# Four residual layers on one Trainium2 core: the norm's row factors inside the first early product, modulation products in groups of four, short fetches elsewhere

## The chip, the core and the metric

The kernel runs on one core of a Trainium2 chip. The metric is the time of one execution in device microseconds. Three runs of the kernel before took 2492.18, 2496.58 and 2499.11 us; the median is 2496.58 us. One further execution was profiled, and all rows below come from it.

## The reference

Four layers work on 256 tokens of 1024 channels; the first two also carry 256 context tokens. Every layer is a mixer and then a gated FFN of width 2816, each behind a modulated RMS norm, with a gated residual sum:

```
m = split(silu(c) @ mod_w[layer] + mod_b[layer], 6)      # shift, scale, gate; shift, scale, gate
h = rms_norm(x, g) * (1 + scale) + shift
x = x + gate * mixer(h)
x = x + gate2 * ((silu(h2 @ w_gate) * (h2 @ w_up)) @ w_down)
```

The mixers are: attention beside a gated linear recurrence (even), retention (odd), and twice a gated delta rule beside window attention, with short convolutions; the FFN of those two has a convolution as well. All is in 32-bit floats. The first two layers need the modulation for two vectors (c and c_ctx), the last two for one.

## The kernel before

A planner orders the work. The program emits instructions with priorities (earlier is more urgent; `high_priority` and `urgent()` raise it, a negative value lowers it), and the planner, with its own costs, puts them into the queues of the engines. Each engine works its queue in order. Nearly all fetches are issued by SyncE, in order, and rotate over eight semaphores; a fetch waits until the one that used its semaphore eight fetches earlier has landed.

**Weights.** `wload` (171) fetches 128 x 1024 floats into one of four `raw` buffers. ScalarE rounds it into `whi` (181), and VectorE, or at every `pool_every`-th load GpSimd, forms the remainder `wlo` (183). A product is three matmuls per block, `mm3` (187 to 192): high x high, low x high, high x low. At the end `wload` calls `fill` (184), which adds `rate` to a credit and, for each whole credit, takes one piece of the modulation from `self.todo`.

**Modulation.** There are three ways. For the first layer's shift and scale, `modulate_first` (1057) multiplies on TensorE at the start. For the rest of the first layer, `mod_round` (337) fetches 128 x 512 floats into one of three `mraw` buffers for each of 8 k and 4 column groups, and multiplies each at once, the 4 groups into 4 different 32-row strips of one bank; it is emitted with low priority in the even mixer. For the other three layers, `mod_sums` (350) does the sum over k as 280 multiply-adds on VectorE (363), after a first scaling on ScalarE (365), and ends each column group with one matmul per vector that sums over the partitions (369). One `yield` is one piece; there are 288. `rate` is 2.9 per weight load in the even layer's FFN, 1.5 in the odd mixer and 1.0 in the odd FFN. `mod_cols` (381) adds the bias and turns the row into columns.

**Norms.** The output product of each part goes channel block by channel block, n = 0 to 7. `norm_block` (504) squares the block on ScalarE (520), adds it to `nsum` on GpSimd (524), and writes the block, scaled but not yet normalized, into hT (527, 528). `norm_scale` (530) then sums over channels with matmuls (537, 538), takes the power -1/2 (540, 541), puts it on a diagonal (545), spreads it to all partitions with matmuls (546) and copies it to `nrs` (548). Meanwhile one or two early products run on the unnormalized hT (`deferred`, 550, with 258 columns, two of them for the shift); their results are multiplied by `nrs` afterwards (`scaled`, 565). `normed` (577) then writes the normalized h over hT in 8 blocks: multiply (587), add the shift and round on ScalarE (588), remainder (589). There are seven such norms after the first one. Squares, scaled results and the products of line 587 share the ring `nt` of five buffers.

**Short fetches.** The head gains `qkg` are fetched at the start (1050), ahead of the vectors (1061), the bias (1068) and the first modulation weights (1078). `swa_heads` (1404 to 1406) and `Delta.gates` (1615, 1616) fetch five small vectors each in each of the last two layers.

Of the kernel before, what the change touches and what calls it, by code (L numbers as in the profile page):

```python
# [19 lines left out]
P = 128  # L20
# [76 lines left out]
class Net:  # L97
# [73 lines left out]
    def wload(self, srcs, a, b):  # L171
# [165 lines left out]
    def mod_round(self, M, r):  # L337

        nc = self.nc
        w, cond = M["w"], self.cond  # L340
        pa = self.bank("mod")
        for k in range(8):
            for g in range(4):
                raw = self.t(self.mpool, [P, 512], tag="mraw", bufs=3)
                c0 = r * 2048 + g * 512
                nc.sync.dma_start(raw, w[k * P:k * P + P, c0:c0 + 512])
                nc.tensor.matmul(pa[32 * g:32 * g + 32], lhsT=cond[:, k, :], rhs=raw, start=k == 0, stop=k == 7)
        self.mod_cols(M, r, pa, range(M["nm"]))

    def mod_sums(self, M, r):  # L350

# [3 lines left out]
        for g in range(4):  # L355
            accs = [self.t(self.mod_pool, [P, 512], tag=f"macc{m}", bufs=1) for m in range(len(vs))]
            for k in range(8):
                raw = self.t(self.mod_pool, [P, 512], tag="mraw2", bufs=2) if k % 5 > 2 else self.t(self.mpool, [P, 512], tag="mraw", bufs=3)
                c0 = r * 2048 + g * 512
                nc.sync.dma_start(raw, M["w"][k * P:k * P + P, c0:c0 + 512])  # L360
                for v, acc in zip(vs, accs):
                    if k:
                        nc.vector.scalar_tensor_tensor(acc, raw, v[:, k:k + 1], acc, ALU.mult, ALU.add)  # L363
                    else:
                        nc.scalar.activation(acc, raw, AF.Copy, scale=v[:, 0:1])  # L365
                if k < 7:
                    yield
            for m, acc in enumerate(accs):
                nc.tensor.matmul(pa[32 * g:32 * g + 32], lhsT=self.ones[:, m], rhs=acc, start=m == 0, stop=m == len(accs) - 1)
            if g == 3:  # L370
                self.mod_cols(M, r, pa, range(len(vs)))
# [9 lines left out]
    def mod_cols(self, M, r, pa, ms):  # L381
# [3 lines left out]
        row = self.t(self.mpool, [P, 512], tag="modrow", bufs=1)  # L385
# [47 lines left out]
    def out_proj(self, y, w, x, gates, rows=None, kbs=None, follow=False, send=None, late=False):  # L433
# [35 lines left out]
        if follow:  # L469
            with self.urgent():  # L470
                self.norm_scale()
# [32 lines left out]
    def norm_block(self, n):  # L504
# [12 lines left out]
        for m, x in enumerate(self.nx):  # L517
            s = slice(m * 256, m * 256 + 256)
            sq = self.t(self.npool, [P, 256], tag="nt", bufs=5) if n else self.nsum[:, s]
# [3 lines left out]
            elif n:  # L523
                nc.gpsimd.tensor_tensor(self.nsum[:, s], self.nsum[:, s], sq, ALU.add)
# [5 lines left out]
    def norm_scale(self):  # L530

        nc, mm = self.nc, self.nc.tensor.matmul
        nt = 2 * len(self.nx)
        ps = self.sm()
        for i in range(nt):
            o = ps[:, 2 * i:2 * i + 2]
            mm(o, lhsT=self.nsum[:, i * P:i * P + P], rhs=self.ones2, start=True, stop=False)
            mm(o, lhsT=self.nsq[i // 2][:, i % 2 * P:i % 2 * P + P], rhs=self.ones2, start=False, stop=True)
# [3 lines left out]
        diag = self.t(self.npool, [P, nt * P], tag="nsum", bufs=1).rearrange("p (i t) -> p i t", t=P)  # L542
        pb = self.sm()
        for i in range(nt):
            nc.vector.tensor_scalar(diag[:, i], self.ident, rs[:, i:i + 1], None, ALU.mult)
# [1359 lines left out]
```

## Time and profile before

| | |
|---|---|
| profiled execution | 2499.45 us |
| its span, first to last instruction | 2497.7 us |
| TensorE (PE) busy | 2372.8 us, 95% |
| VectorE (DVE) busy | 1600.4 us, 64% |
| ScalarE (ACT) busy | 1066.2 us, 43% |
| GpSimd (POOL) busy | 714.9 us, 29% |
| read from HBM | 389.27 MB, 157 GB/s over the span |

A busy TensorE is a pipelined one: neighbouring matmuls overlap in the records, so the shares add up as unions. PEclk is the share of TensorE's clock that was granted. Plain 32-bit matmuls, as in the modulation, leave two records each, the three of `mm3` one each. "Idle before" names what ended an engine's wait.

### The profile page before, as it was taken

How to read it: one execution, taken by the hardware profiler on the slowest of the kernel's cores; microseconds unless marked ns; L12 is line 12 of the kernel's file. 1: busy time of each engine (PE TensorE's matmuls, PEld its weight loads, DVE VectorE, ACT ScalarE, POOL GpSimd, SP SyncE). 2: the span in 40 equal slices, each digit the busy share in tenths (PEclk: the TensorE clock that was granted, in tenths of full speed). 3: DMA queues.
4: the chain of work that ended last, by engine and by line, in shares of the span. 5: the costliest groups of instructions: out<-in, count | busy, mean ns of one | idle time of the engine just before them, and what ended most of it. 6: DMA issues, size and time to landing. Idle time of an engine off the chain costs nothing. (4 is left out here: it accounts for less than half of the span.)

```text
span 2497.7 us, 41691 instructions
## 1 busy us (share of the span) xinstructions
PE 2372.8 (95%) x16388; PEld 2029.3 (81%) x16388; DVE 1600.4 (64%) x2615; ACT 1066.2 (43%) x1744; POOL 714.9 (29%) x537
## 2 busy tenths in 40 slices
PE   6989999999999999998998999998999899999999
PEld 4766658677777788878997887798999787789999
DVE  2676738855656766658545788358765777537773
ACT  2545424332233433334444554235445563345443
POOL 1453423110112112214443453124123352224121
PEclk8999999999999999999998999999999999999999
DMA  7423344566666457556654542245556443245554
GB/s 245 132 89 111 99 132 146 158 198 215 212 219 194 141 174 231 178 181 207 213 178 142 158 122 83 83 140 165 178 183 182 125 134 95 90 139 169 159 180 144
DMA packets 355498, 394.66 MB, mean 158 GB/s; under 512 B 39037, under 2 KB 290861, under 8 KB 355301
## 3 DMA queue, kind: packets, MB, share of 16 engines
q1 hardware_dynamic: 353124, 391.86, 50.9%
q8 instruction: 129, 2.11, 0.3%
q14 instruction: 69, 0.56, 0.1%
q10 hardware_dynamic: 2176, 0.13, 0.1%
HBM read 389.27 MB, written 2.65 MB: 157 GB/s over the span
## 5 line engine op out<-in xcount | busy, mean ns | idle before, releaser
L181 ACT CAST whi<-raw 128x1024 fp32r<-128x1024 f32 (+2 forms) x536 | 553.1, 1033 | 692.4 <-PE acc L191 489.5
L183 DVE TENSOR_TENSOR wlo<-raw,whi 128x1024 fp32r<-128x1024 f32 (+1 forms) x385 | 499.9, 1300 | 375.8 <-ACT whi L181 366.4
L190 PE MATMUL acc<-hTh,whi 128*128 128x256 f32 (+2 forms) x2256 | 695.2, 310 | 20.7 <-ACT hTh L588 15.2
L191 PE MATMUL acc<-hTl,whi 128*128 128x256 f32 (+2 forms) x2256 | 698.4, 310 | 4.6 <-DVE hTl L589 4.4
L192 PE MATMUL acc<-hTh,wlo 128*128 128x256 f32 (+2 forms) x2256 | 696.5, 309 | 1.4 <-DVE wlo L183 1.4
L183 POOL TENSOR_TENSOR wlo<-raw,whi 128x1024 fp32r<-128x1024 f32 (+1 forms) x151 | 363.3, 2406 | 1100.1 <-ACT whi L181 985.6
L190 PEld LDWEIGHTS acc<-hTh,whi 128*128 128x128 f32 x2256 | 433.5, 193 | 59.5 <-ACT hTh L588 16.7
L191 PEld LDWEIGHTS acc<-hTl,whi 128*128 128x128 f32 x2256 | 432.7, 192 | 34.5 <-issue 6.5
L192 PEld LDWEIGHTS acc<-hTh,wlo 128*128 128x128 f32 x2256 | 432.3, 192 | 30.2 <-issue 9.2
L363 DVE SCALAR_TENSOR_TENSOR macc<-mraw,sil,macc 128x512 f32<-128x512 f32 x280 | 233.5, 841 | 48.7 <-ACT macc L365 34.6
L191 PE MATMUL acc<-hidl,whi 128*128 128x256 f32 (+1 forms) x704 | 218.4, 311 | 0.0
L190 PE MATMUL acc<-hidh,whi 128*128 128x256 f32 (+1 forms) x704 | 217.8, 311 | 0.0
L192 PE MATMUL acc<-hidh,wlo 128*128 128x256 f32 (+1 forms) x704 | 217.7, 310 | 0.0
L190 PE MATMUL acc<-whi,hTh 128*128 128x512 f32 (+2 forms) x496 | 182.9, 372 | 13.3 <-ACT hTh L588 12.6
L191 PE MATMUL acc<-wlo,hTh 128*128 128x512 f32 (+2 forms) x496 | 182.5, 369 | 0.0
L192 PE MATMUL acc<-whi,hTl 128*128 128x512 f32 (+2 forms) x496 | 176.7, 366 | 0.0
L190 PEld LDWEIGHTS acc<-hidh,whi 128*128 128x128 f32 x704 | 132.2, 188 | 12.0 <-ACT whi L181 3.4
L191 PEld LDWEIGHTS acc<-hidl,whi 128*128 128x128 f32 x704 | 132.6, 188 | 9.2 <-issue 1.7
L192 PEld LDWEIGHTS acc<-hidh,wlo 128*128 128x128 f32 x704 | 132.6, 188 | 7.8
L190 PEld LDWEIGHTS acc<-whi,hTh 128*128 128x128 f32 x496 | 95.3, 192 | 38.2 <-ACT hTh L588 13.2
L191 PEld LDWEIGHTS acc<-wlo,hTh 128*128 128x128 f32 x496 | 95.5, 193 | 22.4 <-issue 8.0
L192 PEld LDWEIGHTS acc<-whi,hTl 128*128 128x128 f32 x496 | 94.2, 192 | 20.9 <-issue 5.6
(528 smaller groups left out, 3872.9 us busy)
## 6 DMA issues: line engine op xcount, KB each, us to landing
raw<-in_w_in_dram SPq DMA_DIRECT2D x112, 512.0 KB
mraw<-in_w_ada_dram SPq DMA_DIRECT2D x192, 256.0 KB
raw<-in_ffn_w_in_dram SPq DMA_DIRECT2D x88, 512.0 KB
raw<-in_w_up_dram SPq DMA_DIRECT2D x88, 512.0 KB
mraw<-in_mod_w_dram SPq DMA_DIRECT2D x160, 256.0 KB
raw<-in_odd_w_in_dram SPq DMA_DIRECT2D x48, 512.0 KB
raw<-in_ffn_w_out_dram SPq DMA_DIRECT2D x40, 512.0 KB
raw<-in_w_down_dram SPq DMA_DIRECT2D x40, 512.0 KB
```

The lines of the kernel that those rows point to most:

```text
L181: nc.scalar.copy(hi, raw)
L183: eng.tensor_tensor(lo, raw, hi.bitcast(F32), ALU.subtract)
L190: mm(out, lhsT=ah, rhs=bh, start=start, stop=False)
L191: mm(out, lhsT=ah, rhs=bl, start=False, stop=False)
L192: mm(out, lhsT=al, rhs=bh, start=False, stop=stop)
L363: nc.vector.scalar_tensor_tensor(acc, raw, v[:, k:k + 1], acc, ALU.mult, ALU.add)
```

## The change

The norm's row factors are no longer formed at the end of the output product but inside the first early product of the next part: the sums are placed behind its k = 3, the spread behind its k = 7 (`after` adds an order on the queue, without a semaphore). The squares, the scaled results and the products of line 587 get rings of their own (2, 3 and 4 buffers), and the add of block 6 moves from GpSimd to VectorE. Both kinds of modulation products are issued in groups of four that write the four strips of a bank, tied together by `abreast`; `mod_round` fetches 1 MB per k into one buffer, and `mod_sums` has four accumulators and four fetch buffers. `fill` is called by every `mm3` and counts columns, 2048 to a piece, times a rate of 1.3, 1.0 and 1.0. The qkg fetch moves behind the third quarter of the first modulation, the ten small vectors to `setup2`, which runs in the odd layer's FFN. In the odd mixer, the tiles that are first needed after the norm go to a pool that is opened there, `dec` among them. In the last two mixers every second weight remainder goes to GpSimd, up to the values.

```diff
@@ wload, mm3
-        self.fill()
         return hi, lo
...
-        mm(out, lhsT=al, rhs=bh, start=False, stop=stop)
+        last = mm(out, lhsT=al, rhs=bh, start=False, stop=stop)
+        self.fill(int(np.prod(bh.shape[1:])))
+        return last
@@ modulation
+    def after(self, a, b):
+        self.tc.add_manual_dep(a.ins, b.ins.name, mybir.DependencyInfo(mybir.DependencyClass.NoSync, mybir.DependencyReason.DATA), reason="order")
+        return a
+    def abreast(self, mms):
+        last = None
+        for mm in mms:
+            if last is None:
+                last = mm()
+            else:
+                with self.tc.high_priority():
+                    last = self.after(mm(), last)
-    def mod_round(self, M, r):
+    def mod_round(self, M, r, pool):
...
-            for g in range(4):
-                raw = self.t(self.mpool, [P, 512], tag="mraw", bufs=3)
-                c0 = r * 2048 + g * 512
-                nc.sync.dma_start(raw, w[k * P:k * P + P, c0:c0 + 512])
-                nc.tensor.matmul(pa[32 * g:32 * g + 32], lhsT=cond[:, k, :], rhs=raw, start=k == 0, stop=k == 7)
+            raw = self.t(pool, [P, 2048], tag="mraw", bufs=1)
+            nc.sync.dma_start(raw, w[k * P:k * P + P, r * 2048:r * 2048 + 2048])
+            self.abreast([lambda g=g: nc.tensor.matmul(pa[32 * g:32 * g + 32], lhsT=cond[:, k, :], rhs=raw[:, g * 512:g * 512 + 512], start=k == 0, stop=k == 7)
+                          for g in range(4)])
...
+        step = 4 // len(vs)
+        for g0 in range(0, 4, step):
+            gs, accs = range(g0, g0 + step), {}
+            for g in gs:
+                for m in range(len(vs)):
+                    accs[g, m] = self.t(self.mod_pool, [P, 512], tag="macc", bufs=4)
+                for k in range(8):
+                    raw = self.t(self.mod_pool, [P, 512], tag="mraw", bufs=4)
...
+                    if k < 7 or g < gs[-1]:
+                        yield
+            for m in range(len(vs)):
+                self.abreast([lambda g=g: nc.tensor.matmul(pa[32 * g:32 * g + 32], lhsT=self.ones[:, m], rhs=accs[g, m], start=m == 0, stop=m == len(vs) - 1)
+                              for g in reversed(gs)])
...
-    def fill(self):
-        self.credit += self.rate
-        while self.credit >= 1:
-            self.credit -= 1
+    def fill(self, cols):
+        self.credit += self.rate * cols
+        while self.credit >= 2048:
+            self.credit -= 2048
             next(self.todo, None)
@@ out_proj, norm_block, deferred
         if follow:
-            with self.urgent():
-                self.norm_scale()
+            self.nrs = None
...
-            sq = self.t(self.npool, [P, 256], tag="nt", bufs=5) if n else self.nsum[:, s]
+            sq = self.t(self.npool, [P, 256], tag="nsq", bufs=2) if n else self.nsum[:, s]
...
-                nc.gpsimd.tensor_tensor(self.nsum[:, s], self.nsum[:, s], sq, ALU.add)
+                (nc.vector if n == 6 else nc.gpsimd).tensor_tensor(self.nsum[:, s], self.nsum[:, s], sq, ALU.add)
...
+            first = self.nrs is None
...
-                    self.mm3(pa, wh[:, s], wl[:, s], hi[:, k, c], lo[:, k, c], k == 0, k == 7)
+                    last = self.mm3(pa, wh[:, s], wl[:, s], hi[:, k, c], lo[:, k, c], k == 0, k == 7)
+                if first and k in (3, 7):
+                    with self.urgent():
+                        (self.norm_sums if k == 3 else self.norm_spread)(last)
...
-        u, wb = self.t(self.npool, [P, 256], tag="nt", bufs=5), self.col(1, "wb")
+        u, wb = self.t(self.npool, [P, 256], tag="nu", bufs=3), self.col(1, "wb")
...
-                    t = self.t(self.npool, [P, 256], tag="nt", bufs=5)
+                    t = self.t(self.npool, [P, 256], tag="nt", bufs=4)
@@ norm_scale becomes norm_sums (lines 537 to 545) and norm_spread (546 to 548)
+            mm = nc.tensor.matmul(o, lhsT=self.nsum[:, i * P:i * P + P], rhs=self.ones2, start=True, stop=False)
+            self.after(mm, before)
+            before = nc.tensor.matmul(o, lhsT=self.nsq[i // 2][:, i % 2 * P:i % 2 * P + P], rhs=self.ones2, start=False, stop=True)
...
+            mm = nc.tensor.matmul(pb[:, i * P:i * P + P], lhsT=self.onesq, rhs=self.ndiag[:, i], start=True, stop=True)
+            if i == 0:
+                self.after(mm, before)
@@ layer_even, modulate_first
-        for i, n0, n1 in ((0, 0, 8), (1, 8, 10)):
-            self.nc.sync.dma_start(self.qkg[:, n0:n1], I["attn_qk_norm_g"][0, i].unsqueeze(0).unsqueeze(0).to_broadcast([P, n1 - n0, 64]))
...
+            if q == 2:
+                for i, n0, n1 in ((0, 0, 8), (1, 8, 10)):
+                    nc.sync.dma_start(self.qkg[:, n0:n1], I["attn_qk_norm_g"][0, i].unsqueeze(0).unsqueeze(0).to_broadcast([P, n1 - n0, 64]))
@@ odd, setup2, mixer2, swa_heads
+                        o2 = es.enter_context(tc.tile_pool(name="od2", bufs=1, reuse_waits="tile"))
...
+        self.vec2 = [{nm: self.bcast_rows(cp, I[f"{src}_2"][l], w, f"{nm}{l}")
+                      for nm, src, w in (("sgq", "swa_q_norm", 64), ("sgk", "swa_k_norm", 64), ("ssink", "swa_sinks", 16),
+                                         ("alog", "dn_a_log", 8), ("dtb", "dn_dt_bias", 8))} for l in range(2)]
...
+            self.pool_every = 2
...
+                self.pool_every = 4
```

## Rows read from the trace of the kernel before

**Rows 1.** The page, first line: the span.

```profile
span 2497.7 us, 41691 instructions
```

**Rows 2.** Windows: stretch, width, engines' busy us (instructions), PEclk, DMA share, GB/s.

```profile
470.00:830.00 360.00, 360.00 (x1555) 277.54 (x1555) 218.61 (x298) 110.21 (x157) 53.03 (x34) 1.00 0.63 203
```

**Rows 3.** Waits of TensorE: waiter, releaser, total us, times, longest us.

```profile
PE acc L190 <- ACT hTh L588: 27.8, 7, 4.7
PE mod L1083 <- DMA mbig<-in_mod_w_dram: 14.8, 3, 12.9
PE mod L347 <- DMA mraw<-in_mod_w_dram: 2.7, 1, 2.7
```

**Rows 4.** Windows around the seven norms: width, PE busy (instructions), PEclk, DMA share, GB/s.

```profile
435.00:445.00 10.00, 5.46 (x11) 0.66 0.56 177
...
838.00:848.00 10.00, 6.45 (x25) 0.83 0.64 187
1138.00:1165.00 27.00, 20.64 (x123) 0.81 0.51 157
1340.00:1374.00 34.00, 22.04 (x133) 0.80 0.35 98
1736.00:1746.00 10.00, 4.71 (x23) 0.66 0.34 105
1933.00:1944.00 11.00, 6.36 (x18) 0.69 0.29 75
2307.00:2319.00 12.00, 6.70 (x33) 0.72 0.28 88
```

**Rows 5.** TensorE's timeline, 1717 to 1742 us: start, length, what, [idle before].

```profile
1723.23 0.28 PE L190 MATMUL acc<-hTh,whi 128*128 128x258 f32 x1
...
1740.85 0.80 PE L190 MATMUL acc<-hTh,whi 128*128 128x256 f32 x2 [4.60 <-ACT hTh L588]
```

**Rows 6.** VectorE's timeline, 405 to 470 us and 1717 to 1745 us.

```profile
441.65 1.27 DVE L589 SCALAR_TENSOR_TENSOR hTl<-nt,modcols,hTh 128x256 fp32r<-128x256 f32 x3
...
1734.24 0.75 DVE L569 TENSOR_TENSOR nt<-acc,nrs 128x256 f32<-128x256 f32 x2 [1.92 <-ACT nrs L548]
...
1739.79 0.47 DVE L587 SCALAR_TENSOR_TENSOR nt<-x,moda,nrs 128x256 f32<-128x256 f32 x1
```

**Rows 7.** TensorE's timeline, 68 to 110 us and 296 to 352 us.

```profile
76.01 1.06 PE L347 MATMUL mod<-mraw,cond 128*32 128x512 f32 x6
...
318.31 1.05 PE L347 MATMUL mod<-mraw,cond 128*32 128x512 f32 x2
319.29 0.39 PE L191 MATMUL acc<-wlo,hTh 128*128 128x256 f32 x1
```

**Rows 8.** Lines by form, TensorE: records, busy us, mean ns, idle before.

```profile
L347 PE MATMUL mod<-mraw,cond 128*32 128x512 f32 x128 | 44.4, 618 | 2.7 <-DMA mraw<-in_mod_w_dram 2.7
L369 PE MATMUL mod<-macc,ones 128*32 128x512 f32 x80 | 43.7, 635 | 2.6 <-DVE macc L363 2.2 <-DVE modcols L396 0.4
```

**Rows 9.** Windows: the end of the even mixer.

```profile
300.00:352.00 52.00, 49.34 (x316) 26.79 (x316) 25.79 (x63) 11.93 (x26) 21.17 (x25) 0.97 0.47 145
```

**Rows 10.** Windows: two stretches of the start.

```profile
15.00:20.00 5.00, 0.00 (x0) 0.00 (x0) 0.00 (x0) 0.00 (x0) 0.00 (x0) 0.80 0.06 17
...
35.00:40.00 5.00, 2.69 (x31) 1.19 (x27) 3.50 (x9) 3.03 (x5) 0.00 (x0) 0.85 1.09 352
```

**Rows 11.** SyncE's timeline, 0 to 64 us.

```profile
4.17 1.66 SPq L1050 DMA_DIRECT2D qkg<-in_attn_qk_norm_g_dram  x2
...
9.78 14.57 SPq L1068 DMA_DIRECT2D mbias<-in_mod_b_dram  x4
```

**Rows 12.** Waits of SyncE's queue.

```profile
SPq L1068 <- DMA qkg<-in_attn_qk_norm_g_dram: 11.8, 2, 11.2
```

**Rows 13.** The timeline of all engines, 1700 to 1746 us.

```profile
1707.73 0.21 DVE L1409 TENSOR_TENSOR sgk<-sgk,sgq 128x48 f32<-128x48 f32 x1 [2.46 <-DMA sgk<-in_swa_k_norm_dram]
```

**Rows 14.** The page's costliest groups: weight remainders on GpSimd.

```profile
L183 POOL TENSOR_TENSOR wlo<-raw,whi 128x1024 fp32r<-128x1024 f32 (+1 forms) x151 | 363.3, 2406 | 1100.1 <-ACT whi L181 985.6
```

More of the change, by code (lines that the diff above doesn't have):

```diff
@@ L354, in mod_sums @@
         vs = M["vs"][:M["nm"] if r == 0 else 1]
[L355 to L371, printed above, removed]
+        step = 4 // len(vs)
@@ new lines, in mod_sums @@
+        for g0 in range(0, 4, step):
[5 more added lines that the diff above has]
+                    raw = self.t(self.mod_pool, [P, 512], tag="mraw", bufs=4)
+                    c0 = r * 2048 + g * 512
+                    nc.sync.dma_start(raw, M["w"][k * P:k * P + P, c0:c0 + 512])
+                    for m, v in enumerate(vs):
+                        if k:
+                            nc.vector.scalar_tensor_tensor(accs[g, m], raw, v[:, k:k + 1], accs[g, m], ALU.mult, ALU.add)
+                        else:
+                            nc.scalar.activation(accs[g, m], raw, AF.Copy, scale=v[:, 0:1])
+                    if k < 7 or g < gs[-1]:
[3 more added lines that the diff above has]
+                              for g in reversed(gs)])
+            if gs[-1] == 3:
+                self.mod_cols(M, r, pa, range(len(vs)), self.t(self.mod_pool, [P, 512], tag="mraw", bufs=4))
@@ L528, in norm_block, with norm_sums @@
             nc.vector.scalar_tensor_tensor(lo[:, n, c], x[:, n], a, hi[:, n, c].bitcast(F32), ALU.mult, ALU.subtract)
-    def norm_scale(self):
-        nc, mm = self.nc, self.nc.tensor.matmul
+    def norm_sums(self, before):
+        nc = self.nc
         nt = 2 * len(self.nx)
@@ L541, in norm_scale, with norm_spread @@
         nc.gpsimd.tensor_tensor(rs, v, self.neghalf[:, 0:nt], ALU.pow)
-        diag = self.t(self.npool, [P, nt * P], tag="nsum", bufs=1).rearrange("p (i t) -> p i t", t=P)
+        self.ndiag = self.t(self.npool, [P, nt * P], tag="nsum", bufs=1).rearrange("p (i t) -> p i t", t=P)
+        for i in range(nt):
+            nc.vector.tensor_scalar(self.ndiag[:, i], self.ident, rs[:, i:i + 1], None, ALU.mult)
+    def norm_spread(self, before):
+        nc = self.nc
+        nt = 2 * len(self.nx)
         pb = self.sm()
         for i in range(nt):
-            nc.vector.tensor_scalar(diag[:, i], self.ident, rs[:, i:i + 1], None, ALU.mult)
-            mm(pb[:, i * P:i * P + P], lhsT=self.onesq, rhs=diag[:, i], start=True, stop=True)
+            mm = nc.tensor.matmul(pb[:, i * P:i * P + P], lhsT=self.onesq, rhs=self.ndiag[:, i], start=True, stop=True)
+            if i == 0:
+                self.after(mm, before)
         self.nrs = self.t(self.npool, [P, nt * P], tag="nrs")
@@ L644, in ffn @@
                 self.out_proj(lambda k, t0, t1: tuple(v[:, k % 2, t0:t1] for v in hid[k // 2]), w_out, x, gates,
-                              kbs=[2 * j + fb for j in js for fb in range(2)], follow=end and follow is not None, send=send)
+                              kbs=[2 * j + fb for j in js for fb in range(2)], follow=end and follow is not None, send=send and (lambda n: send(n, pool)))
     def conv_act(self, conv, a, pa, blk):
@@ L1144, in even_ffn @@
         self.ffn(512, I["ffn_w_in"][0], I["ffn_w_out"][0], x, [self.gate(M, m, 5) for m in range(2)],
-                 (x, lambda: [self.modpair(M1["cols"], m, 0, 1, self.vcol("ng", 2)) for m in range(2)]), rate=2.9)
+                 (x, lambda: [self.modpair(M1["cols"], m, 0, 1, self.vcol("ng", 2)) for m in range(2)]), rate=1.3)
     def odd(self, x, M, done):
@@ L1152, in odd @@
         TBS = [0, 1, 2, 3]
-        with tc.tile_pool(name="od", bufs=1, reuse_waits="tile") as op:
+        with tc.tile_pool(name="od", bufs=1, reuse_waits="tile") as op, ExitStack() as es:
+            o2 = None
             rope = self.const(op, "rope")
@@ L1194, in odd @@
                         done()
-                        self.rate = 1.5
+                        self.rate = 1.0
+                        o2 = es.enter_context(tc.tile_pool(name="od2", bufs=1, reuse_waits="tile"))
+                    if hd % 2 == 0:
+                        yh, yl = (self.t(o2, [P, 8, 256], F32R, tag=nm, bufs=1) for nm in ("oyh", "oyl"))
+                    dec = self.t(o2, [P, 4, 256], tag="dec", bufs=1)
+                    nc.sync.dma_start(dec, I["k_dec"][:, hd * 1024:hd * 1024 + 1024].rearrange("p (s t) -> p s t", s=4))
+                    vh, vl = (self.t(o2, [P, 4, 512], F32R, tag=nm, bufs=1) for nm in ("ovh", "ovl"))
                     values()
                     (qh, ql), (kh, kl) = fm["q"], fm["k"]
-                    ph, pl = (self.t(op, [P, 4, 256], F32R, tag=nm, bufs=1) for nm in ("oph", "opl"))
+                    ph, pl = (self.t(o2, [P, 4, 256], F32R, tag=nm, bufs=1) for nm in ("oph", "opl"))
                     for s2 in range(2):
@@ L1403, in swa_heads @@
         nc, I = self.nc, self.I
-        gq = self.bcast_rows(ap, I["swa_q_norm_2"][l], 64, "sgq")
-        gk = self.bcast_rows(ap, I["swa_k_norm_2"][l], 64, "sgk")
-        sink = self.bcast_rows(ap, I["swa_sinks_2"][l], 16, "ssink")
+        gq, gk, sink = (self.vec2[l][nm] for nm in ("sgq", "sgk", "ssink"))
         nsink = self.t(ap, [P, 16], tag="snsink")
```

29 lines of the change are left out of this document (10 added, 19 removed).

## Prediction

> **What bounds the kernel now.** I read the page first, then the granted clock and busy times by stretches, then who waited for whom on TensorE, and last the timelines of the stretches with gaps. The profiled execution took 2499.45 us around a span of 2497.7 us [rows 1]; the three timed runs have a median of 2496.58, 1 us below that span. My sum is made against the span, and that 1 us is taken off. TensorE is the engine that sets the time: long stretches have no gap at all (360.00 of 360 us, beside 218.61 on VectorE) [rows 2]. What is left to gain is therefore of two kinds: work taken off TensorE, and the gaps, which the list of waits names. Two stand out: seven waits, 27.8 us, for the re-normalized activations (line 588), and one of 12.9 us at the start for the first modulation weights [rows 3]. [...]
>
> **Norms.** In the seven stretches of [rows 4] TensorE is idle 4.5 + 3.6 + 6.4 + 12.0 + 5.3 + 4.6 + 5.3 = 41.7 us. The clock takes (1 - share) x width, 3.4 + 1.7 + 5.1 + 6.8 + 3.4 + 3.4 + 3.4 = 27.2 us, less the half speed that lies inside the gaps themselves; I estimate that at a quarter, so 20. Together 62 us: the most that this part can give.
> How much comes back is read from one norm, at 1723 us. Two early products fill TensorE from 1723.2 to 1736.2, and then it waits 4.60 us [rows 5]. VectorE gets the row factors (nrs) at 1734.2, spends 5.5 us on evacuating the early products, and starts the first line-587 operation at 1739.8 [rows 6]. So two things are late: the factors, and the first 587 behind the evacuation; `nt` is one ring of five shared by squares, scaled results and 587, so 587 also has to wait for those to be consumed. The change ties the sums behind k = 3 and the spread behind k = 7 of the first product. A product is 13/2 = 6.5 us, so the factors can exist some 7.5 us after its start, at 1730.7, 3.5 us earlier. With rings of their own, four 587s can run at once, and they are urgent. From then on VectorE needs two operations for each k; three of them in a row take 1.27 us [rows 6], so 0.85 us per k and 6.8 for eight. The second product frees hT block by block from about 1730.6, so the norm can end near 1737.5, and the next product, starting at 1736.2, wants its last block some 2.8 us in (7 steps of 6.5/16, since it takes its two column halves one after the other). No gap is due, and the evacuation is what is late next; it lies beside the next product as long as a PSUM bank is free.
> The two norms with 512 columns (435, 838) need twice that, 13.6 us; there I take half of the loss, (4.5 + 3.6 + 0.75 x 5.1)/2 = 6 us, and of the other five, 50 us, four fifths. The norm at 1340 loses most because its chain stands alone before the bank layout changes: the products of the next layer could not start under it. Now they are its cover. Forced order is the new risk: the first sum queues all of TensorE behind nsum. The last add goes from GpSimd to VectorE, which shortens that wait; a miss costs what it misses, at most the present gaps. Taken: 6 + 39 = 45 us, bounds 0 and 62.
>
> **Modulation products.** Each [32 x 512] product appears as two records. One alone spans 1.05 us, and three whose outputs are in different 32-row groups span 1.06 us [rows 7]: they already run side by side when they happen to be neighbours. Behind a lone one the successor starts after 0.98 us [rows 7]. Line 369 has 80 records, 40 products, 43.7 us [rows 8]: 1.09 each, so nearly all are alone. After: eight rounds with one vector, one group of four each; the round with two vectors, two pairs for each of two vectors: 12 slots of about 1.0 us. So 40 x 0.98 - 12 = 27 us. Their stretch is the gap-free one [rows 2], with VectorE and DMA (0.63) below full, so all but 1 is taken: 26, bounds 15 and 28. The VectorE multiply-adds and the bytes stay as they are. Pieces now follow columns: 1.3 x 233,472/2048 = 148 in the FFN, 90 in the odd mixer, 51 in its FFN, together 289 for 288 pieces; so none is late. Four accumulators instead of one per vector only take waits from ScalarE.
> Line 347 has 128 records, 44.4 us [rows 8]; at 1.05 that is 42 slots for 64 products, some being neighbours. After: 16 groups of four; 42 x 0.98 - 16 = 25 us. Here the stage decides. In 300 to 352 us TensorE has 49.3 of 52 us, VectorE 25.8, GpSimd 21.2 [rows 9]; with the products gone, TensorE would have about 80%, and part of the chains of scan, softmax and state would show through. I take 16, nearest to a full TensorE; bounds -5 and 25.
> That round's fetch changes too: 1 MB into a single buffer in place of 256 KB into three. Nothing in the trace shows such a fetch. At 352 GB/s, the start's rate [rows 10], 1.05 MB takes 3.0 us; beside the 145 GB/s of [rows 9] it takes 1.05/0.207 = 5.1. Behind a waiting fetch SyncE's queue holds all weight loads; four weight buffers cover. Sixteen times 5.1 + 1 is 98 us; from the first of these products, at 76 us [rows 7], to the norm at 435 there is room for that. The lower bound of -5 is one such wait in the open.
> [...]
>
> **Short fetches.** The two qkg broadcasts are issued at 4.2 us; the fourfold bias fetch behind them then occupies SyncE from 9.8 to 24.35 [rows 11], 11.8 us of it waiting for qkg [rows 12], while the DMA engines are 0.06 busy, one of sixteen [rows 10]. Only then can the first modulation weights leave. Without qkg ahead this wait goes: up to 12.9 us of TensorE gap [rows 3] and 2 us of clock. But qkg does not get shorter. It moves into the stretch in which DMA is saturated (1.09) [rows 10]; there SyncE can meet the same wait some fetches later, and loads behind it wait for its one engine. I take half: 8 us, bounds -5 and 15.
> [...]
> The small vectors of the second block go to the FFN before it. Until 1707.7 VectorE waited 2.46 us for sgk, with the evacuation that frees TensorE's banks behind it [rows 13]; that goes, and its twin in the other such layer: 2 us, bounds 0 and 5. Their ten issues lie under a full TensorE. dec moves behind the norm, and is wanted a whole product later: 0.
>
> **GpSimd's share.** In each second-block mixer 35 weight splits now go every second, not every fourth, to GpSimd: some 18 more in all, each 2.4 us there [rows 14]. VectorE is relieved, and GpSimd also carries the chain of the triangular inverse. I take 0; half of 18 x 2.4, 20 us, bounds it on either side.
>
> **Sum.** 45 + 26 + 16 + 8 + 2 = 97 us. The order of every queue is planned anew, so gaps outside these places will move; I take off 12 for new ones, some three norm gaps. 2497.7 - 85 = 2413 for the span, 2412 for the median.
>
> **Rivals.**
> First, VectorE binds the norms: evacuation, splits and the two operations per k are there whenever nrs comes. Then a third of 62 returns, 24 us less than taken: 2436. For it: VectorE takes 0.85 us per k where a column half of a product takes 0.4; against it: 5.5 us of evacuation stood ahead of the norm.
> Second, filler: the 347 products only filled the even stage, and qkg's time moves with it; 24 us less: 2436. Both together: 2460.
> Third, all bounds reached but the GpSimd share: 62 + 28 + 25 + 15 + 5 = 135: 2362.
> Fourth, slower: TensorE meets each of the sixteen 1 MB groups before its data. Its queue is in order, so every product behind waits 5.1 + 1 us, and the clock drops after gaps of this length as it does after the norm's 4.6; 16 x (6.1 + 2) = 130 us, in place of the 16 gained. With 81 - 12 of the rest: 2497.7 + 130 - 69 = 2559. It decides from 69/16 = 4.3 us each, a fetch that is nearly never early. For it: one buffer; against it: the present fetches made TensorE wait once, 2.7 us [rows 3].
> That the change does not do what it says (groups of four torn apart by the planner) is inside the second.
>
> **Chances.** Forecast 0.50, first rival 0.16, second 0.16, both 0.05, third 0.07, slower 0.06. Less than 0.3% (7.5 us), about what a measurement can tell from none, would need nearly every term to fail. Faster 0.90, same 0.04, slower 0.06. The range 2374 to 2464 takes in the two rivals together and stops short of the third, which needs every bound at once.
>
> **What would show it.** Right: waits of TensorE for line 588 below 10 us; granted clock above 0.9 in the norm stretches; the modulation products in runs of eight records that span about 1.1 us; first modulation product near 14 us; no sgk wait. Wrong: a new row of TensorE waiting for nsum or mraw, or SyncE waiting for qkg again with TensorE idle behind it.

## The result and the profile after

The changed kernel takes 2422.8 us (median of four runs, 2417.6 to 2423.5) against 2496.1 us before: a ratio of 0.970 with a 95% interval of 0.968 to 0.972, 73 us less. The forecast was 2412 us, its range 2374 to 2464. The total came out as forecast to within 11 us; its terms did not, and the experiments below show which were wrong. (Lines of the changed kernel have new numbers: 548 is now 576, 569 is 601, and 587 to 589 are 619 to 621.)

The page after begins so (span; busy time of each engine, its share, instructions):

```profile
span 2420.2 us, 41624 instructions
...
PE 2305.9 (95%) x16388; PEld 2017.7 (83%) x16388; DVE 1613.3 (67%) x2607; ACT 1063.9 (44%) x1748; POOL 756.3 (31%) x545
```

The span fell by 77.5 us from that of [rows 1]. TensorE's busy time fell by 66.9 us (2372.8 on the page before) and the rest of its span, its idle time, by 10.6. So most of the gain is work that TensorE no longer does or does at a higher clock (a mean granted clock of 0.972 before, 0.980 after), and the smaller part is gaps. These are the modulation products (lines by form, records, busy us, mean ns; then one group of four in the timeline):

```profile
L361 PE MATMUL mod<-mraw,cond 128*32 128x512 f32 x128 | 17.1, 604 | 1.7 <-DMA mraw<-in_mod_w_dram 1.7
L389 PE MATMUL mod<-macc,ones 128*32 128x512 f32 x80 | 12.3, 603 | 0.0
```

```profile
95.06 1.06 PE L361 MATMUL mod<-mraw,cond 128*32 128x512 f32 x8
```

Against [rows 8] that is 27.3 and 31.4 us less, 58.7 of the 66.9. A group of eight records, four products, spans 1.06 us, where one product alone spanned 1.05 in [rows 7]. The middle of the first FFN has no gap, as in [rows 2]:

```profile
440.00:780.00 340.00, 340.00 (x1514) 273.08 (x1512) 214.97 (x283) 108.02 (x155) 49.53 (x30) 1.00 0.64 203
```

The waits of TensorE, to be read beside [rows 3], and the seven norms, beside [rows 4] (busy us of PE, PEld, DVE, ACT, POOL, then PEclk, DMA share, GB/s):

```profile
PE acc L189 <- DVE nu L601: 10.2, 6, 5.3
...
PE acc L190 <- DVE hTl L621: 7.9, 6, 2.6
...
PE sm L189 <- ACT araw L1167: 4.4, 1, 4.4
PE mod L1113 <- issue: 4.3, 1, 4.3
...
PE mod L361 <- DMA mraw<-in_mod_w_dram: 1.7, 1, 1.7
```

```profile
397.00:407.00 10.00, 4.69 (x25) 4.72 (x26) 10.00 (x16) 3.61 (x8) 2.50 (x1) 0.66 0.67 209
799.00:809.00 10.00, 7.56 (x31) 5.58 (x31) 10.00 (x23) 4.47 (x10) 1.99 (x2) 1.00 0.64 185
1096.00:1123.00 27.00, 21.94 (x160) 19.56 (x158) 22.80 (x57) 13.88 (x27) 6.39 (x3) 0.94 0.47 141
1294.00:1317.00 23.00, 20.87 (x133) 18.64 (x134) 19.30 (x35) 11.78 (x25) 9.63 (x6) 1.00 0.51 139
1667.00:1677.00 10.00, 5.90 (x41) 5.29 (x40) 10.00 (x22) 5.57 (x11) 1.19 (x2) 0.95 0.29 94
1863.00:1877.00 14.00, 9.85 (x41) 7.05 (x42) 14.00 (x29) 8.54 (x19) 6.38 (x2) 1.00 0.22 59
2231.00:2241.00 10.00, 5.61 (x37) 4.99 (x36) 10.00 (x20) 5.42 (x12) 2.76 (x1) 0.91 0.35 108
```

Of the wait for the high parts of a norm, 27.8 us before, one of 2.3 us is left, and another has taken its place: TensorE waits for VectorE, either to evacuate an early product (line 601) or for the low parts (line 621; 7.9 and 2.2 us, 4.4 before). In these windows TensorE is idle 104 - 76.4 = 27.6 us, in those of before 41.7. The clock is better in six of seven. The longest wait left at a norm, 5.3 us at 397, is in the window that still averages 0.66 in clock.

VectorE is busy 10.00 of 10 or 14.00 of 14 us in five of these windows. That alone is not new: [rows 4] show TensorE only, but with all engines three of their windows read so, among them these two (VectorE is the third engine):

```profile
1736.00:1746.00 10.00, 4.71 (x23) 4.00 (x21) 10.00 (x25) 7.19 (x15) 0.61 (x2) 0.66 0.34 105
...
2307.00:2319.00 12.00, 6.70 (x33) 6.20 (x32) 12.00 (x28) 8.00 (x16) 2.70 (x1) 0.72 0.28 88
```

What changed shows in the 12 us behind the factors, summed over the seven norms, before and then after:

```profile
sum 84.00, PE 61.52 PEld 54.64 DVE 70.25 ACT 50.12 POOL 16.72; mean PE 8.79 PEld 7.81 DVE 10.04 ACT 7.16 POOL 2.39
```

```profile
sum 84.00, PE 64.62 PEld 55.63 DVE 83.88 ACT 52.19 POOL 21.78; mean PE 9.23 PEld 7.95 DVE 11.98 ACT 7.46 POOL 3.11
```

Before, VectorE still had pauses in which it waited; after, it works without one (83.88 of 84 us). That it now binds the norms is what the experiments below test.

The time between the ends of the copies of the norm factors (line 548, after 576), cut into one stage up to each norm and one behind the last, shows where the 77.5 us lie:

| stage up to the factors of | before, us | after, us | difference |
|---|---|---|---|
| even FFN (start and even mixer) | 420.8 | 397.6 | -23.2 |
| odd mixer (even FFN) | 409.5 | 389.1 | -20.4 |
| odd FFN (odd mixer) | 318.9 | 311.9 | -7.0 |
| second block, layer 1 mixer | 202.0 | 202.2 | +0.2 |
| its FFN | 383.0 | 363.8 | -19.2 |
| layer 2 mixer | 196.9 | 197.2 | +0.3 |
| its FFN | 373.5 | 366.7 | -6.8 |
| the end | 193.1 | 191.7 | -1.4 |

At the start, the first modulation product comes at 14.6 us, as forecast. But SyncE's timeline shows a hold-up like that of [rows 11] some 26 us later:

```profile
6.06 5.45 SPq L1098 DMA_DIRECT2D mbias<-in_mod_b_dram  x4
11.56 3.99 SPq L1108 DMA_DIRECT2D mbig<-in_mod_w_dram  x8
...
25.34 6.94 SPq L1108 DMA_DIRECT2D mbig<-in_mod_w_dram  x8
32.67 2.17 SPq L1117 DMA_DIRECT2D qkg<-in_attn_qk_norm_g_dram  x2
...
36.11 15.02 SPq L1108 DMA_DIRECT2D mbig<-in_mod_w_dram  x6
```

Six fetches behind qkg take 15.0 us to issue, where each run of eight ahead of it took 4.0 to 6.9, and TensorE has gaps of 4.4 and 4.3 us at 50 and 57 us (the waits for araw and the one called issue above). It is not the wait of [rows 12] again: SyncE waits only 0.3 us for qkg to land, but the first two of the six issues last 8.84 and 3.53 us by themselves. Meanwhile the DMA engines are 0.11 busy, less than two engines of sixteen, as they were 0.06 busy in [rows 10]:

```profile
36.00:45.00 9.00, 8.63 (x101) 7.11 (x101) 3.20 (x9) 2.08 (x4) 0.00 (x0) 1.00 0.11 28
```

### The profile page after: what moved, and what is told of

Read it like the earlier page. It is cut to its first block, busy times and chain, and to the rows that moved or that the text cites. A ratio compares the mean times of both kernels' runs of the same rounds, so it can differ in the third digit from the quotient of the medians.

```text
span 2420.2 us, 41624 instructions
## 1 busy us (share of the span) xinstructions
PE 2305.9 (95%) x16388; PEld 2017.7 (83%) x16388; DVE 1613.3 (67%) x2607; ACT 1063.9 (44%) x1748; POOL 756.3 (31%) x545
## 4 chain that ended last, share of the span: by engine, by line
PE 76%; DVE 11%; DMA 6%; issue 3%; POOL 2%; ACT 1%; SPq 1%; DVEq 0%; POOLq 0%; ACTq 0%
PE acc L191 21%; PE acc L190 21%; PE acc L189 21%; DMA mraw<-in_w_ada_dram 2%; DVE macc L383 2%; DVE wlo L183 1%; PE rc L1640 1%; DVE nt L619 1%; DVE hTl L621 1%; PE sm L1873 1%; PE rc L1861 1%; DMA mbig<-in_mod_w_dram 1%; DMA raw<-in_even_w_in_dram 1%; PE sm L1875 1%; PE rc L1863 1%
## 5 line engine op out<-in xcount | busy, mean ns | idle before, releaser
L183 POOL TENSOR_TENSOR wlo<-raw,whi 128x1024 fp32r<-128x1024 f32 (+1 forms) x168 | 411.8, 2451 | 1091.3 <-ACT whi L181 1006.7
L183 DVE TENSOR_TENSOR wlo<-raw,whi 128x1024 fp32r<-128x1024 f32 (+1 forms) x368 | 481.0, 1308 | 306.2 <-ACT whi L181 299.8
L383 DVE SCALAR_TENSOR_TENSOR macc<-mraw,sil,macc 128x512 f32<-128x512 f32 x280 | 247.7, 894 | 82.2 <-DMA mraw<-in_w_ada_dram 43.0
L191 PEld LDWEIGHTS acc<-whi,hTl 128*128 128x128 f32 x496 | 93.6, 191 | 20.4 <-DVE hTl L621 4.5
```

Of the source, the lines that this page charges most:

```text
L183: eng.tensor_tensor(lo, raw, hi.bitcast(F32), ALU.subtract)
L191: last = mm(out, lhsT=al, rhs=bh, start=False, stop=stop)
L383: nc.vector.scalar_tensor_tensor(accs[g, m], raw, v[:, k:k + 1], accs[g, m], ALU.mult, ALU.add)
```

## The experiments

Each kernel was timed four or five times beside the kernel before, whose medians were 2495.1 to 2497.1 us; the ratios are to that. The theory under test was the prediction's own sum. Its main rival, the prediction's first, is that VectorE binds the norms; a second one was read from the two traces: that the whole norm edit is worth at most the 19 us that the products leave of the 77.5.

| run | edit of the changed kernel | us | against 2422.8 | ratio to before |
|---|---|---|---|---|
| norm_at_end | binding undone | 2430.7 | +7.8 | 0.974 (0.972 to 0.976) |
| shared_ring | rings undone | 2443.4 | +20.6 | 0.978 (0.977 to 0.980) |
| norm_before | both undone | 2450.5 | +27.7 | 0.982 (0.980 to 0.984) |
| sums_lone | sums' products apart | 2459.7 | +36.8 | 0.985 (0.982 to 0.987) |
| rounds_lone | rounds as before | 2439.2 | +16.4 | 0.977 (0.975 to 0.979) |
| qkg_start | qkg at the start | 2424.9 | +2.1 | 0.971 (0.969 to 0.973) |
| pool_4 | GpSimd's share as before | 2416.2 | -6.6 | 0.968 (0.966 to 0.969) |
| norm_no_lo | no low parts in norms | 2396.9 | -25.9 | 0.960 (0.958 to 0.961) |
| sums_behind | sums behind the norm | 2404.8 | -18.0 | 0.964 (0.962 to 0.965) |
| qkg_once | qkg once a row | 2408.8 | -14.0 | 0.965 (0.963 to 0.967) |
| best | the last two | 2393.0 | -29.8 | 0.958 (0.956 to 0.959) |
| best_quiet | and no GpSimd splits at norms | 2377.6 | -45.3 | 0.952 (0.951 to 0.953) |

Two intervals of half width 0.002 make a difference uncertain by some 6 to 7 us; so the 2 us of qkg_start are no difference that was measured, the 7.8 and 6.6 barely are, and the others are.

**The norm.** norm_at_end puts the factors back behind the projection:

```diff
         if follow:
-            self.nrs = None
+            with self.urgent():
+                self.norm_scale()
...
-(nc.vector if n == 6 else nc.gpsimd).tensor_tensor(self.nsum...
+nc.gpsimd.tensor_tensor(self.nsum...
```

> The changed kernel with the norm's factors computed as before, in one piece at the end of the preceding output projection; the rings of their own, the products four abreast and all else stay. Theory of the prediction: the binding is what brings the norms' 45 us, so this kernel takes about 2423 + 45 = 2468 us (2452 to 2485). Theory of the two traces: idle time of TensorE fell by only 11 us over the whole kernel, and the busy time outside the modulation products by 8 us, so the binding and the rings together are worth at most about 19 us: 2435 to 2442. Rival (VectorE binds the norms whenever the factors come): under 8 us, 2423 to 2430.

It cost 7.8 us: neither 45 nor up to 19, but what the rival allowed. So the rings were tried, with the binding undone (norm_before) and with it kept (shared_ring):

```diff
-tag="nsq", bufs=2   -tag="nu", bufs=3   -tag="nt", bufs=4
+tag="nt", bufs=5    +tag="nt", bufs=5   +tag="nt", bufs=5
```

> The changed kernel with the whole norm edit undone: the factors in one piece at the end of the projection, and one ring of five for squares, scaled results and the first normalizing operation. Prediction: 45 us slower than the changed kernel, 2468 us. Theory of the traces (idle time of TensorE down by 11 us, its busy time outside the modulation products by 8): about 15 to 20 us slower, 2438 to 2443, that is 7 to 12 above the kernel with the binding alone undone (2431). Rival (VectorE binds the norms whatever the rings and the binding): no more than the 8 us that the binding alone gave, 2431.

> The changed kernel with the binding kept and one ring of five in place of the three rings. Undoing the binding alone cost 8 us, undoing both 28. If the rings carry 20 us whatever the binding: 2443. If either edit alone brings nearly all (the ring only matters when the factors come late): 2423 to 2428. If the rings do nothing without the binding, and the binding nothing without the rings: 2450.

Both undone cost 27.7 us, the rings alone 20.6: the parts add up (28.4), and the larger is the rings. So the prediction's 45 is too much, the 15 to 20 read from the traces too little, and the rival's 8 is out for the rings. About half of the 27.7 goes with the clock and is not in the gaps: by the profiled executions TensorE is idle 127.2 us in norm_before against 114.3, and busy 2320.2 against 2305.9 with the same products, at a mean granted clock of 0.969 against 0.980. In shared_ring the old wait is back, by its list of waits and, at one norm, VectorE's timeline:

```profile
PE acc L189 <- ACT hTh L620: 26.2, 8, 5.5
```

```profile
1685.70 0.76 DVE L601 TENSOR_TENSOR nt<-acc,nrs 128x256 f32<-128x256 f32 x2 [1.00 <-ACT nrs L576]
...
1693.04 1.26 DVE L619 SCALAR_TENSOR_TENSOR nt<-x,moda,nrs 128x256 f32<-128x256 f32 x3
```

The factors are there at 1685.7, and the first normalizing operation (line 619) starts 7.3 us later, behind the evacuation whose buffers it shares. In the changed kernel four of them start at once, at 1664.62, as the factors come. The two edits do not need each other: early factors are worth 7.1 us with one ring (2450.5 to 2443.4) and 7.8 with three, both at the edge of what can be told.

norm_no_lo leaves out the low parts (line 621) of every norm:

> The changed kernel without the last VectorE operation of each block of a norm (line 621): the low parts of the normalized activations stay those of the block before normalization. It leaves out 176 VectorE operations of 0.4 us in all seven norms, 70 us of VectorE work, and no work of TensorE. Theory (VectorE binds the norms after the change: it is busy 10.00 of 10 us there): most of the 31 us of TensorE gaps at the norms go, and some of the clock, 20 to 35 us faster, 2390 to 2403. Rival (the chain sums, factors, ScalarE's high parts binds): the gaps stay within 8 us, 2415 or more.

There are 72 such operations, 34.9 us by the list of lines, not 176 and 70 us. It was 25.9 us faster, in the range of the theory. The seven norms, each from 6 us ahead of the factors to 20 behind them, first in the changed kernel and then without the low parts; behind them two single windows of the latter:

```profile
sum 182.00, PE 155.07 PEld 141.07 DVE 155.11 ACT 91.25 POOL 47.29; mean PE 22.15 PEld 20.15 DVE 22.16 ACT 13.04 POOL 6.76
```

```profile
sum 182.00, PE 172.24 PEld 161.64 DVE 156.74 ACT 109.02 POOL 51.81; mean PE 24.61 PEld 23.09 DVE 22.39 ACT 15.57 POOL 7.40
```

```profile
1656.00:1666.00 10.00, 9.27 (x76) 8.89 (x75) 9.05 (x17) 7.75 (x16) 2.45 (x2) 1.00 0.34 109
...
2211.00:2221.00 10.00, 10.00 (x87) 10.00 (x86) 9.70 (x19) 8.07 (x18) 2.78 (x1) 1.00 0.37 117
```

With one of VectorE's two operations per block gone, TensorE's idle time at the norms falls from 26.9 to 9.8 us; VectorE stays as busy, with the work that follows. This edit also takes away the last link of the chain, TensorE's wait for the low parts (10.1 us), so by itself it does not tell VectorE's load from that link. Two things do: outside the first norm the waits for an evacuation (line 601), which does not use the low parts, fall from 4.9 to 2.0 us; and sums_behind, below, only moves other work out of VectorE's way, and the gap at the first norm is gone. Together with the 83.88 of 84 us above: VectorE binds the norms.

**The modulation products.** sums_lone issues each column group's products when its sum is ready; rounds_lone has 256 KB fetches and lone products again:

```diff
-        step = 4 // len(vs)
+        step = 1
```

```diff
-            raw = self.t(pool, [P, 2048], tag="mraw", bufs=1)
...
+            for g in range(4):
+                raw = self.t(pool, [P, 512], tag="mraw", bufs=3)
```

> The changed kernel with the reducing products of the modulation sums issued one column group at a time, as each group's sum is finished, in place of two or four side by side; fetches, VectorE work and pieces stay. Prediction: 26 us slower, 2449. Traces: busy time of that line fell from 43.7 to 12.3 us under a full TensorE, so 31 us slower, 2454. Rival (the products only fill time in which TensorE would wait anyway): under 5 us.

> The changed kernel with the two modulation rounds in the even mixer as before: 256 KB fetches into three buffers and products placed one by one. Prediction: 16 us slower, 2439. Traces: the line's busy time fell by 27 us and the stage up to the first norm by 26 us, so about 25 us slower, 2448. Rival (filler): within 5 us of the changed kernel; by the rival of the single buffer it would be faster than the changed kernel.

Their lines by form, first of sums_lone, then of rounds_lone:

```profile
L389 PE MATMUL mod<-macc,ones 128*32 128x512 f32 x80 | 35.0, 604 | 0.0
```

```profile
L363 PE MATMUL mod<-mraw,cond 128*32 128x512 f32 x128 | 38.9, 605 | 0.0
```

Apart, they take 22.7 and 21.8 us more of TensorE. The rounds give 16.4 us of their 21.8, all in the first stage (414.4 against 397.6): some of it was filler, as the prediction had it. The sums cost 36.8 us by the medians and 24.0 by the spans of the profiled executions (2444.2 and 2420.2); the profiled one is the shortest of that kernel's five, the others being 2459 to 2463 at a mean clock of 0.974 to 0.976 in place of 0.982. So some 23 us are the products themselves; the rest goes with the lower clock, whose cause no trace here shows. In the profiled one the loss lies where the sums run, 20.0 us in the even FFN's stage, nearly all that the change had gained there, and 9.9 in the odd mixer's; the other stages are 5.9 us shorter together. The rivals of filler alone and of the single buffer are out: TensorE waited once, 1.7 us, for a 1 MB fetch.

**qkg.** qkg_start moves its two broadcasts back; qkg_once leaves them at their new place, but fetches each row once, and VectorE spreads it over the heads:

```diff
             if q == 2:
-                for i, n0, n1 in ((0, 0, 8), (1, 8, 10)):
-                    nc.sync.dma_start(self.qkg[:, n0:n1], ... .to_broadcast([P, n1 - n0, 64]))
+                nc.sync.dma_start(self.qkg2, I["attn_qk_norm_g"][0].unsqueeze(0).to_broadcast([P, 2, 64]))
...
         gain = self.qkg
+        for i, n0, n1 in ((0, 0, 8), (1, 8, 10)):
+            nc.vector.tensor_copy(gain[:, n0:n1], self.qkg2[:, i:i + 1].to_broadcast([P, n1 - n0, 64]))
```

> The changed kernel with the two qkg broadcasts issued at the start again, ahead of the modulation bias. Prediction: 8 us slower, 2431. Theory of the traces: TensorE's gaps before 80 us sum to 23.3 us in the kernel before and 16.0 us in the changed one, where SyncE spends 15.0 us on six modulation fetches behind qkg, so the move gave back half of what it took away: 5 to 8 us slower. [...]

> The changed kernel with qkg fetched once for each of its two rows, at the same place (one DMA with 512 bytes for a partition, in place of two with 2560), and spread over the heads by two VectorE copies in the even mixer. Theory (the small packets of the repeated rows on one DMA engine hold up SyncE, and so the last modulation fetches, and make the gaps of 4.4 and 4.3 us at 50 and 57): both gaps go, 8 to 12 us faster, 2411 to 2415. Rival (these gaps are those of a start that is bound by the bytes that it fetches): within 3 us, 2420 to 2426.

The move is worth nothing that can be measured: the first stage takes 397.5 us with qkg at the start and 397.6 without. (By the traces TensorE's gaps before 80 us, behind its first product, sum to 20.8 us in the kernel before, 17.0 in the changed one and 19.1 in qkg_start, so the move makes a difference of 2; the 23.3 and 16.0 above do not come out.) The smaller fetch is worth 14 us, slightly more than its theory gave. SyncE's timeline of qkg_once, and a window of it:

```profile
31.92 0.35 SPq L1118 DMA_DIRECT2D qkg<-in_attn_qk_norm_g_dram  x1
...
33.48 4.34 SPq L1110 DMA_DIRECT2D mbig<-in_mod_w_dram  x6
```

```profile
33.00:45.00 12.00, 11.63 (x117) 9.34 (x116) 4.07 (x12) 3.07 (x6) 2.38 (x1) 1.00 1.08 359
```

The six fetches behind it take 4.3 us, not 15.0, and the DMA engines stay full (1.08, where the changed kernel has 0.11); both gaps of TensorE are gone from its list of waits, and the factors of the first norm come at 384.3 us, not 397.6. The later stages stay within 2.6 us of those of the changed kernel. One DMA in place of two, fewer bytes and fewer small pieces come together here; which of them counts was not tried.

**What stands in VectorE's queue.** sums_behind orders every multiply-add of the modulation sums behind the norm's last operation:

```diff
-                            nc.vector.scalar_tensor_tensor(accs[g, m], ...)
+                            self.after(nc.vector.scalar_tensor_tensor(accs[g, m], ...), self.last_norm)
```

> The changed kernel with every VectorE multiply-add of the modulation sums ordered behind the last operation of the norm before it, so that none of them can stand between the factors and the norm. Theory (the filler on VectorE in front of the norm makes the gap of 5.3 us at 397 and the clock loss behind it): 4 to 9 us faster, 2414 to 2419. Rival (the sums are late then and TensorE waits for them, or the gap has another cause): same or slower, 2421 to 2435.

It gave 18 us, twice what was expected: 4 in the even FFN's stage (385.2 against 389.1), 11 in the odd mixer's (300.7 against 311.9), which I had not counted. Two other stages moved by +3.9 us (206.1) and, where no sum is left, by -5.9 (360.8): the queues are planned anew, and this is the size that a stage can move by that alone. At the first norm, VectorE's and then GpSimd's timeline of the changed kernel, and then VectorE's and a window of sums_behind:

```profile
396.08 4.16 DVE L383 SCALAR_TENSOR_TENSOR macc<-mraw,sil,macc 128x512 f32<-128x512 f32 x3
400.17 0.47 DVE L619 SCALAR_TENSOR_TENSOR nt<-x,moda,nrs 128x256 f32<-128x256 f32 x1
```

```profile
397.20 2.50 POOL L183 TENSOR_TENSOR wlo<-raw,whi 128x1024 fp32r<-128x1024 f32 x1 [4.86 <-ACT wb L600]
```

```profile
397.38 0.48 DVE L619 SCALAR_TENSOR_TENSOR nt<-x,moda,nrs 128x256 f32<-128x256 f32 x1 [3.57 <-ACT nrs L576]
```

```profile
396.00:406.00 10.00, 10.00 (x86) 10.00 (x85) 4.32 (x9) 5.80 (x10) 2.40 (x1) 1.00 0.18 53
```

The filler stood in front of the norm in VectorE's queue, although the norm is urgent. With it behind, TensorE has no gap at that norm and the full clock.

best joins this with qkg_once; best_quiet also keeps GpSimd from the next ten weight splits at each norm:

```diff
-        eng = nc.gpsimd if self.gran % self.pool_every == 0 else nc.vector
+        eng = nc.gpsimd if self.gran % self.pool_every == 0 and self.quiet <= 0 else nc.vector
+        self.quiet -= 1
...
+        if self.nrs is None:
+            self.quiet = 10
         wt = self.wfm(w, c0)
```

> The changed kernel with both edits that gained: the multiply-adds of the modulation sums ordered behind the norm, and qkg fetched once for each of its rows. Theory (two separate places, 397 us and later, and 50 to 60 us): the gains of 18 and 14 us add up, 2423 - 32 = 2391 us (2386 to 2396). Rival (part of each gain is the new planning of the queues, or the first makes up for what the second brings): 2397 to 2405.

> The kernel of the run best, with GpSimd kept from the next ten weight splits from the first product of each norm on; VectorE does them, some two or three of 1.2 us more for each norm. Theory (a VectorE operation on SBUF that meets one of GpSimd's splits of 2.4 us is held until that ends, as at 1664.6 us, where four operations of 0.47 us take 3.80): each norm gets 1 to 2 us back, 5 to 12 us faster than best. Rival (VectorE binds the norms by the count of its operations, and the splits only add to it): 3 to 10 us slower than best.

The two gains add up (2393.0, where the sum is 2390.8), and quieting GpSimd brings 15.4 us more, though it gives VectorE more to do. The four operations that open a norm, in the changed kernel with GpSimd's split beside them, in best, and in best_quiet; then, for best and for best_quiet, the whole line and the engines' busy time:

```profile
1664.62 3.80 DVE L619 SCALAR_TENSOR_TENSOR nt<-x,moda,nrs 128x256 f32<-128x256 f32 x4 [1.04 <-ACT nrs L576]
```

```profile
1665.75 2.39 POOL L183 TENSOR_TENSOR wlo<-raw,whi 128x1024 fp32r<-128x1024 f32 x1 [4.72 <-ACT whi L181]
```

```profile
1640.70 3.81 DVE L619 SCALAR_TENSOR_TENSOR nt<-x,moda,nrs 128x256 f32<-128x256 f32 x4 [1.05 <-ACT nrs L576]
```

```profile
1633.00 1.67 DVE L622 SCALAR_TENSOR_TENSOR nt<-x,moda,nrs 128x256 f32<-128x256 f32 x4 [1.04 <-ACT nrs L577]
```

```profile
L619 DVE SCALAR_TENSOR_TENSOR nt<-x,moda,nrs 128x256 f32<-128x256 f32 x56 | 31.5, 593 | 12.4 <-ACT nrs L576 12.4
```

```profile
PE 2297.9 (96%) x16388; PEld 2012.4 (84%) x16388; DVE 1623.4 (68%) x2609; ACT 1060.6 (44%) x1746; POOL 757.2 (32%) x545
```

```profile
L622 DVE SCALAR_TENSOR_TENSOR nt<-x,moda,nrs 128x256 f32<-128x256 f32 x56 | 25.5, 485 | 9.0 <-ACT nrs L577 9.0
```

```profile
PE 2291.2 (97%) x16388; PEld 2005.4 (84%) x16388; DVE 1613.4 (68%) x2634; ACT 1060.2 (45%) x1746; POOL 697.0 (29%) x520
```

In both kernels with the split beside them, the four operations last until it has ended, at 1668.1 us in the changed one. VectorE does 25 operations more in best_quiet and is busy 10.0 us less, so the rival, the count of operations, is out. How much of the 15 us this is stays open: the largest part, 6.5 us, lies in the second block's first stage, where best was 8.1 us longer than the changed kernel (210.3, then 203.8, against 202.2), so part of it may be the new planning.

pool_4 undoes the same kind of share elsewhere, in the mixers of the second block:

```diff
-            self.pool_every = 2
```

> The changed kernel with GpSimd's share of the weight splits left at every fourth in the mixers of the second block, as before. Prediction: no difference (0, with 20 us on either side). Theory of the stages (these mixers kept their length where no norm lies in them, 193.1 against 191.7 us and 196.9 against 197.2): within 5 us, 2418 to 2428. Rival (the share is part of the 19 us that the stage up to 1734 us gave back): 10 us or more slower.

It is 6.6 us faster, within the prediction's 20, just outside the theory's range, not the way of the rival, and at the edge of what can be told: GpSimd's larger share gained nothing and probably costs time. 4.1 us lie in one of the two mixers' stages (366.7 us); the other (363.8) is 0.8 us longer, and the rest lies in stages that the edit does not touch.

## Why the prediction was right in its total and wrong in its terms

**Norms: 45 taken, 28 measured.** The step that failed is "No gap is due": TensorE is still idle 27.6 us in the seven windows. The step gave VectorE nothing but the norm's own operations from the moment the factors came. It had evacuations, weight splits, sums in its queue and operations held up beside GpSimd (3.80 us for four at 1664.62), and was busy without a pause (83.88 of 84 us); that it was already full in windows of the kernel before could have been read there. The first rival named this mechanism; with a third of 62, 21 us, its price is nearer to 28 than 45 is. Right was that two things were late, the factors and the first normalizing operation behind the evacuation; but I priced them as one, and the second, the rings, is worth 20.6 us and the first 7.8. Right too was to count the clock beside the gaps: about half of the 27.7 us goes with it, and in windows of 1 us of the trace before the granted clock is 1.00 up to 1738 us and 0.50 from 1739 to 1745, around the wait of [rows 5]: the half speed that the estimate of 20 us uses. The forced order cost little: TensorE waits 0.8 us for nsum in the sums and 1.1 in the spread. (In the working, four fifths of 50 are 40, not 39.)

**Sums: 26 taken, 37 by medians, 24 by the profiled spans.** The count of slots and the full TensorE were right; the median over the runs is larger, with a lower clock.

**Rounds: 16 taken, 16.4 measured.** Here the weighing of saved work against a stage that is partly filler held: 27 us of busy time gone, and gaps of 4.8 and 1.9 us at 322 and 330 us in place of 3.2. Of the 23.2 us of the first stage, rounds_lone takes back 16.8, norm_before 2.2 and qkg_start nothing; the other 4 are not traced to an edit.

**Start: 8 taken, 2 measured, nothing that can be told from none.** The second rival's part of this came about, and with it a sign named for being wrong, SyncE held behind qkg with TensorE idle: TensorE's wait at 14 us went and its twins appeared 35 and 42 us later. I put half where nothing was left; the half was an estimate that no run shows. What the runs show is that the fetches behind qkg are held up at either place, by 11.8 us of waiting in [rows 12] and with 15.0 us for six issues in the changed kernel, while the DMA engines are 0.06 and 0.11 busy; what holds the six up no row shows.

**GpSimd: 0 taken, a loss of 6.6 measured, barely more than can be told.** Its own time was bounded; that VectorE is held up beside its splits (3.80 us for four operations that take 1.67 in best_quiet) was not thought of.

**Short vectors: 2 taken.** The two waits for sgk, 6.0 us of VectorE's, are gone from its list; what that is worth by itself was not tried, nor were the new count of `fill` and the new pool in the odd mixer.

**Twelve taken off for new gaps.** The undone parts sum to 27.7 + 36.8 + 16.4 + 2.1 - 6.6 = 76.4 us against 73.3 measured, so no such reserve shows. With the sums at 24 the parts make 64, and 10 us have no part of their own. The total agreed by luck: norms, start and GpSimd, 30 us too high together, stand against the sums and the reserve, 23 too low. What is left between 76 and 73 is within the uncertainty of the parts.

## What to carry to other kernels

Before pricing an earlier start of a chain, read how busy the engine is that carries the chain: here an urgent operation still stood behind filler in its queue (18.0 us) and behind the buffers of its ring (20.6 us). Give rings of their own first; order fillers behind the chain by hand. Here a small fetch that its access pattern repeats held up the large ones behind it: shrinking it gave 14.0 us, moving it nothing. After each edit of such a planned program expect other stages to move by some 4 to 6 us.

## Behaviour of the hardware that was not expected

**VectorE and GpSimd get in each other's way.** Of line 383 in the changed kernel, the 224 records that meet no GpSimd operation last at most 0.76 us; of the 56 that meet one, 31 last over 0.9 us, and the longest 2.94. Of the 38 that meet a weight split, 24 began after it and end 0.55 us after it; 13 began before it and take their usual 0.75. The rows at 1664.62 us fit these 37: 3.80 us for four operations of 0.47 beside a split of 2.39, where the four take 1.67 in best_quiet, with no split beside them. The other way round, a split at 1869.8 us, among VectorE's operations of a norm, lasts 6.27 us where the line's mean is 2.45. By what the two hold each other up no trace here shows. So a split beside it cost one operation of line 383 up to 2.2 us (2.94 against 0.76) and the four of a norm 2.1 (3.80 against 1.67), and where VectorE binds that is time.

**Four narrow products side by side cost what one does:** 1.05 us for one alone in [rows 7], 1.06 or 1.07 us for eight records in fifteen of the sixteen groups of the rounds, the sixteenth (1.13) being cut in two by the records of another product, and 1.06 or 1.07 in eight of the ten groups of the sums. The other two are those of the round with two vectors, two pairs one after the other, and take 1.91.
